# One queue for the opening's transfers, six row buffers, and an earlier third key projection, in a hybrid encoder layer

## The chip, the core and the metric

The kernel runs on one core of a Trainium2 chip. The core has a matrix engine, TensorE (PE in the profile, with its weight loads as PEld), a vector engine (DVE), a scalar engine for activations and copies (ACT), a general engine (POOL, GpSimd), and a sync engine (SP) that mostly issues transfers. Each engine works through its own list of instructions in order; semaphores hold an instruction until its operands are there. Transfers (DMA) between device memory and the on-chip memory can be issued from SP, ACT or POOL, each with its own queue, and sixteen DMA engines carry them out. Matmuls accumulate in PSUM, a small memory from which ACT and DVE must take the results ("evacuate") before a buffer can be used again.

The metric is the time of one execution in device microseconds.

## The reference

One encoder layer is applied to two groups of tokens with the same weights, 256 "prompt" and 512 "sample" tokens, 768 in all, model width 1024. In short:

```python
h = rmsnorm(x, norm_mix_g)
u, q, k, v, qm, gl = split(h @ w_in)
s5_out   = S5 state-space mixer of u, half-GLU
diff_out = differential attention of q, k, v
mem_out  = memory_attention(qm, rmsnorm(mem, mem_norm_g), w_mem_kv)
merged = sum of sigmoid(gl + b_gate) * (branch @ w_branch)
x = x + merged @ w_out
x = x + (silu(g) * up) @ w_down       # h2 = rmsnorm(x), SwiGLU
```

The change concerns the beginning: the normalisation of `mem` (256 memory rows for each group) and of `x`, and the projections of the memory branch. It has four heads of width 256. For head i there is a key projection `("k", i)` and a value projection `("v", i)` of the normalised memory, and a query projection `("q", i)` of the normalised input `h`. All arithmetic is in float32; for the matmuls each operand is split into a high and a low part in a rounded format, and three products of the parts replace one.

## The kernel before

**Weights.** A class `WStream` holds a list of weight blocks in the order in which they are used; a block of 1024 x 256 comes in two halves of 512 KB. `_dma` (line 556) issues one half from SP into one of three raw buffers (`wr`), `_split` (line 650) makes its high part on ACT (`wh`, line 665) and its low part on DVE (`wl`, line 671), into pools of four buffers each, and `get`/`ahead` (lines 673 to 694) keep the stream ahead of use. A raw buffer is free for the next transfer when its low part is made; a `wh` buffer is free when the matmuls that read it are done.

**The order of the memory branch** stands in a list:

```python
MEM_ORDER = [("k", 0), ("k", 1), ("v", 0), ("v", 1), ("q", 0), ("k", 2), ("q", 1), ("v", 2), ("k", 3), ("q", 2),
             ("v", 3), ("q", 3)]
```

`mem_k` (line 929) projects a head's keys with 96 matmuls of 256 columns, in four tiles of tokens, each evacuated by ACT into `kr` (line 940) and squared (line 942). `mem_v` (line 946) first normalises the keys of its head on DVE, then projects the values, with evacuation `Vh`/`Vl` scaled by the row factor `mrs` of the memory. `mem_q` (line 965) projects the queries from the normalised input `H` (tiles `mq`), with 48 matmuls of 256 columns for the prompt and 48 of 512 for the sample, evacuates into `mqh`/`mql`, and transposes the keys (`kT`). Result tiles of these projections take turns in three PSUM buffers (`psd`).

**The opening** (lines 1063 to 1140) is a block of its own:

- `memT`, the transposed memory, comes in four pieces (`mt`, tag `ft`, four buffers) from SP, between the weight halves. It is multiplied by the gain column `gcols` and split into `memThi`/`memTlo` (lines 825, 826); the first key projection runs along with the splitting (line 1088).
- The row factors of the memory need sums of squares of four rows tiles (`load_row`, line 854; squares on DVE, line 1094), and those of the input six (squares on ACT, `square_sum`, line 849, with a separate result tile `njk`). All ten tiles are loaded from POOL's queue into one tag `row` of two buffers.
- `xT`, the transposed input, comes in four pieces (line 1121) from POOL into the same four `ft` buffers as `memT`.
- The input's row factors are spread over all partitions by matmuls (`rsb`, line 1132). Then DVE multiplies `xT` by gain and factor (line 1136), ACT makes `Hhi` (line 822) and DVE `Hlo` (line 823).
- The projections `("k", 1)`, `("v", 0)`, `("v", 1)` are a generator `rest()` whose steps are taken between these parts.

**Behind the opening** a loop (line 1147) goes through `MEM_ORDER[4:]`. It is interleaved with two other generators by `Pace`: `mem_attend` (line 994), the attention of heads whose projections are done, and `s5.params` (line 58), a long chain of small DVE operations on 128 x 64 tiles with a few on ACT, which computes the parameters of the S5 mixer. They advance with each unit of the loop except those of `("q", 0)`. The small tiles of `s5.params` without a name take turns in a ring of 12 buffers. The gate bias `bg` (line 1160) and the gain `subg` (line 1251) are loaded from SP; they are used at lines 1210 and 1261, in later stages.

**What sets the order.** The program is handed to a scheduler that places instructions within each engine's list by its own estimate of time; only those passed through `tc.keep_in_program_order` stay where they are written. So a transfer that waits for nothing can be placed far ahead of the line that issues it. This is why `bg` and `subg` stand eighth and ninth in SP's list.

## Time and profile before

| | |
|---|---|
| median of 3 runs | 1765.29 us (1763.75 to 1769.2) |
| the profiled execution | 1769.52 us, of which its span 1767.7 us |
| PE busy in the span | 1723.5 us (97%) |
| DVE busy | 1341.6 us (76%) |
| ACT busy | 934.6 us (53%) |
| POOL busy | 301.0 us (17%) |
| device memory read, written | 173.51 MB, 52.17 MB |

The span runs from the first to the last instruction of the profiled execution; times in the rows below are microseconds from its start. A row of the windows view gives for a stretch A:B its length, then the busy time of each engine with its number of instructions, the granted TensorE clock (1.00 is full speed), the mean busy share of the sixteen DMA engines, and GB/s. A row in order of time gives start, duration, engine, line, operation, result and operands, and in brackets the idle time of the engine before it with what ended it; "SPq" rows are the queue of SP, whose duration is how long issuing took. A row of the waits view reads: who waited for whom, total, number, longest. Line numbers are those of the kernel before. A matmul's busy time overlaps that of the next, so busy PE is not PE at full flow; counts show that better.

### The profile page before, as it was taken

The page shows a single profiled execution, that of the slowest core. Times are in us where ns is not written, and L with a number is a line of the kernel's source. Part 1 is how long each engine was busy: PE and PEld are TensorE (multiplying, and loading weights), DVE is VectorE, ACT ScalarE, POOL GpSimd, SP SyncE. Part 2 cuts the span into 40 slices and gives each one's busy share as a digit, 9 for nine tenths or more (in the row PEclk, how much of TensorE's full clock was granted, in tenths as well). Part 3 has the DMA queues.
Part 4 walks back from the last instruction along what each step waited for, and adds up shares of the span by engine and source line. Part 5 has one row for each costly group of instructions (what it writes and reads, how often), then busy time and mean ns, then how long its engine had stood idle before and what let it go on. Part 6 is the DMA issues. An engine that isn't in the chain of part 4 may idle for free.

```text
span 1767.7 us, 29778 instructions
## 1 busy us (share of the span) xinstructions
PE 1723.5 (97%) x11312; PEld 1589.3 (90%) x11312; DVE 1341.6 (76%) x2453; ACT 934.6 (53%) x1909; POOL 301.0 (17%) x324
## 2 busy tenths in 40 slices
PE   7699999999999999999999999999999999999999
PEld 7699988888888899999988899898889898989897
DVE  3786575899899645898976687895578868787866
ACT  4535453667566436778866554553334544444541
POOL 1000000000000001011110020350023333443420
PEclk8899999999999999999999999999999999999999
DMA  8412245676666525666594255564303546575743
GB/s 269 155 51 96 90 146 153 148 178 179 165 174 172 146 83 122 142 150 137 145 221 129 93 168 185 148 157 164 104 25 96 149 108 170 139 170 131 167 121 111
DMA packets 202174, 249.90 MB, mean 141 GB/s; under 512 B 33584, under 2 KB 155472, under 8 KB 202032
## 3 DMA queue, kind: packets, MB, share of 16 engines
q1 hardware_dynamic: 156496, 147.18, 27.3%
q0 software_dynamic: 34592, 75.67, 21.1%
q10 hardware_dynamic: 10944, 25.17, 4.1%
q8 instruction: 89, 1.46, 0.3%
q14 instruction: 53, 0.43, 0.1%
HBM read 173.51 MB, written 52.17 MB: 128 GB/s over the span
## 4 chain that ended last, share of the span: by engine, by line
PE 76%; issue 15%; DMA 3%; DVE 3%; ACT 2%; POOL 1%; SPq 0%; POOLq 0%; DVEq 0%; ACTq 0%
PE br L831 4%; PE br L830 4%; PE br L832 4%; PE up L830 3%; PE up L831 3%; PE up L832 3%; PE gate L831 3%; PE gate L830 3%; PE gate L832 3%; PE dn L830 3%; PE dn L831 3%; PE dn L832 3%; PE qk L832 3%; PE qk L830 3%; PE qk L831 3%
## 5 line engine op out<-in xcount | busy, mean ns | idle before, releaser
L665 ACT ACTIVATE wh<-wr 128x1024 fp32r<-128x1024 f32 x118 | 133.8, 1135 | 79.0 <-PE gl L831 19.2
L671 DVE TENSOR_TENSOR wl<-wr,wh 128x1024 fp32r<-128x1024 f32 x72 | 96.2, 1337 | 74.0 <-ACT wh L665 72.3
L830 PE MATMUL gl<-Hhi,wh 128*128 128x256 f32 (+1 forms) x384 | 133.2, 347 | 0.0
L832 PE MATMUL gl<-Hhi,wl 128*128 128x256 f32 (+1 forms) x384 | 129.4, 337 | 0.0
L831 PE MATMUL gl<-Hlo,wh 128*128 128x256 f32 (+1 forms) x384 | 129.4, 337 | 0.0
L669 POOL DMA_DIRECT2D wl<-wr x46 | 40.1, 881 | 465.2 <-ACT wl L668 452.0
L830 PE MATMUL qk<-wh,Hhi 128*128 128x256 f32 x384 | 108.1, 282 | 0.0
L831 PE MATMUL qk<-wl,Hhi 128*128 128x256 f32 x384 | 108.0, 281 | 0.0
L832 PE MATMUL qk<-wh,Hlo 128*128 128x256 f32 x384 | 107.7, 281 | 0.0
L590 DVE TENSOR_TENSOR wl_S<-ws,wh_S 128x512 fp32r<-128x512 f32 x91 | 67.4, 763 | 27.0 <-ACT wh_S L585 26.7
L585 ACT ACTIVATE wh_S<-ws 128x512 fp32r<-128x512 f32 x91 | 54.1, 625 | 63.4 <-PE up L831 27.0
L830 PEld LDWEIGHTS gl<-Hhi,wh 128*128 128x128 f32 x384 | 72.2, 188 | 10.2 <-issue 2.2
L832 PEld LDWEIGHTS gl<-Hhi,wl 128*128 128x128 f32 x384 | 72.3, 188 | 9.2 <-issue 0.6
L831 PEld LDWEIGHTS gl<-Hlo,wh 128*128 128x128 f32 x384 | 72.4, 188 | 7.5
L830 PEld LDWEIGHTS qk<-wh,Hhi 128*128 128x128 f32 x384 | 72.1, 188 | 0.9
L832 PEld LDWEIGHTS qk<-wh,Hlo 128*128 128x128 f32 x384 | 72.2, 188 | 0.5
L831 PEld LDWEIGHTS qk<-wl,Hhi 128*128 128x128 f32 x384 | 72.2, 188 | 0.5
L1378 DVE TENSOR_REDUCE nm<-sc 128x1 f32<-128x512 f32 (+1 forms) x96 | 56.8, 599 | 14.6 <-PE sc L1373 13.8
L1380 ACT ACTIVATE p<-sc,nm 128x512 f32<-128x512 f32 (+1 forms) x96 | 59.0, 617 | 11.0 <-DVE nm L1378 10.6
L611 POOL TENSOR_TENSOR ws<-wr,ws 128x512 f32<-128x512 f32 x26 | 39.9, 1536 | 123.4 <-DVE wl_S L590 119.7
L585 ACT ACTIVATE wh_A<-wr 128x512 fp32r<-128x512 f32 x65 | 38.0, 623 | 37.1 <-PE up L831 16.0
L590 DVE TENSOR_TENSOR wl_A<-wr,wh_A 128x512 fp32r<-128x512 f32 x57 | 51.8, 931 | 6.4 <-ACT wh_A L585 6.4
(705 smaller groups left out, 6244.6 us busy)
## 6 DMA issues: line engine op xcount, KB each, us to landing
wr<-in_w_in_dram SPq DMA_DIRECT2D x48, 512.0 KB, 4.5
wl<-wr POOLq DMA_DIRECT2D x46, 512.0 KB, 5.4
wr<-in_w_gate_up_dram SPq DMA_DIRECT2D x44, 512.0 KB, 4.3
wr<-in_w_branch_dram SPq DMA_DIRECT2D x24, 512.0 KB, 3.5
wr<-in_w_down_dram SPq DMA_DIRECT2D x22, 512.0 KB, 4.6
wr<-in_w_mem_kv_dram SPq DMA_DIRECT2D x16, 512.0 KB, 3.7
wr<-in_w_in_dram SPq DMA_DIRECT2D x32, 256.0 KB, 4.4
p_scr<-de ACTq DMA_DIRECT2D x27, 256.0 KB, 3.9
```

The source lines that it names most:

```text
L585: self.nc.scalar.activation(f(hi), src, AF.Copy)
L590: self.nc.vector.tensor_tensor(out=f(lo), in0=src, in1=f(hi).bitcast(F32), op=ALU.subtract)
L611: gt(out=s4, in0=A12, in1=s2, op=sub)
L665: self.nc.scalar.activation(hi, r, AF.Copy)
L669: self.nc.gpsimd.dma_start(lo, r.bitcast(F32R), accum_op=ALU.add)
L671: self.sub.tensor_tensor(out=lo, in0=r, in1=hi.bitcast(F32), op=ALU.subtract)
L830: pe.matmul(ps, wh, xh, start=start, stop=False)
L831: pe.matmul(ps, wh, xl, start=False, stop=False)
L832: pe.matmul(ps, wl, xh, start=False, stop=stop)
L1378: v.tensor_reduce(out=nm[:, m : m + 1], in_=ps, axis=AX.X, op=ALU.max, negate=True)
L1380: act.activation(pm[:, 0:n], ps, AF.Exp, bias=nm[:, m : m + 1], accum_out=s1s[:, tt : tt + 1] if m == 0 else s2)
```

## The change

- The rows, `xT` and the two gains `gk`, `gq` are issued from SP and not from POOL; `gcols` from ACT. The transfers of the opening, including the weight halves in it (`W.pin`), stay in program order. `bg` and `subg` stay in program order too, so they are issued behind the projections and in the stage of the differential attention.
- The weight stream is brought to four halves ahead of the memory rows. The memory rows are loaded together, before the keys of head 0 are evacuated, and squared behind that.
- A row goes either to the two buffers `row` or to one of the four `ft` buffers. The square of an input row is written over the row itself.
- `("k", 2)` stands ahead of `("q", 0)` and belongs to the opening's generator. `kr` has three buffers instead of two.
- The matmuls that spread the row factors are kept in program order.
- To make room, the ring of `s5.params` has 9 buffers instead of 12, and three of its named tiles share the space of others (`dt` with `ldt`, `thr` with `th`, `p8i` with `xr`).
- The tile `ones2` is filled by DVE instead of POOL.

```diff
@@ S5.params
-            return scratch.tile([128, w], dt, name=nm, tag="ring", bufs=12)
+            return scratch.tile([128, w], dt, name=nm, tag="ring", bufs=9)
-        dt = t("dt")
+        dt = ldt
-        thr = reduce_2pi(t("thr"), th)
+        thr = reduce_2pi(th, th)
-        p8i, p8r = sincos(th8, t("p8i"), t("p8r"))
+        p8i, p8r = sincos(th8, xr, t("p8r"))
@@ WStream
+        self.pin = lambda i: i
-            self.nc.sync.dma_start(tv[:, :, n * j : n * j + n], a[:, k2 * h : k2 * h + k2, :])
+            self.pin(self.nc.sync.dma_start(tv[:, :, n * j : n * j + n], a[:, k2 * h : k2 * h + k2, :]))
@@ hybrid_block
-    MEM_ORDER = [("k", 0), ("k", 1), ("v", 0), ("v", 1), ("q", 0), ("k", 2), ("q", 1), ("v", 2), ("k", 3), ("q", 2),
+    MEM_ORDER = [("k", 0), ("k", 1), ("v", 0), ("v", 1), ("k", 2), ("q", 0), ("q", 1), ("v", 2), ("k", 3), ("q", 2),
-    def square_sum(x, pool, ss):
-        jk = pool.tile([128, 1024], F32, name=uid("njk"), tag="njk", bufs=1)
-        return act.activation(jk, x, AF.Square, accum_out=ss)
-    def load_row(pool, src, eng):
-        x = pool.tile([128, 1024], F32, name=uid("row"), tag="row", bufs=2)
-        eng.dma_start(x, src)
+    def square_sum(x, ss):
+        return act.activation(x, x, AF.Square, accum_out=ss)
+    def load_row(pool, src, ft):
+        if ft:
+            x = pool.tile([128, 2 * TOK], F32, name=uid("row"), tag="ft", bufs=4)[:, 0:1024]
+        else:
+            x = pool.tile([128, 1024], F32, name=uid("row"), tag="row", bufs=2)
+        W.pin(nc.sync.dma_start(x, src))
         return x
-        kr = k1.tile([128, 4, 256], F32, name=uid("kr"), tag="kr", bufs=2)
+        kr = k1.tile([128, 4, 256], F32, name=uid("kr"), tag="kr", bufs=3)
+        W.pin = pin = tc.keep_in_program_order
+        nc.scalar.dma_start(cg, A["gcols"])
-        gp.memset(ones2, 1.0)
+        v.memset(ones2, 1.0)
+        def features(src, n):
+            def load(j):
+                t = pool.tile([128, 2 * TOK], F32, name=uid("ft"), tag="ft", bufs=4)
+                t = t[:, 0 : 2 * n].rearrange("p (k t) -> p k t", k=2)
+                pin(nc.sync.dma_start(t, src[:, 2 * j : 2 * j + 2]))
+                return t
+            return load
+        mt, xt = features(A["memT"], 512), features(A["xT"], TOK)
         W._dma()
-        mt = []
-        for j in range(4):
-            if j == 2:
-                W._dma()
-            t = pool.tile([128, 2 * TOK], F32, name=f"mt{j}", tag="ft", bufs=4)
-            t = t[:, 0:1024].rearrange("p (k t) -> p k t", k=2)
-            nc.sync.dma_start(t, A["memT"][:, 2 * j : 2 * j + 2])
-            if j == 0:
-                nc.gpsimd.dma_start(cg, A["gcols"])
-            mt.append(t)
+        fm = [mt(0), mt(1)]
+        W._dma()
+        fm += [mt(2), mt(3)]
...
+        while W.n_dma < 4:
+            W._dma()
+        rm = [load_row(pool, ms[t], t > 1) for t in range(4)]
         W.get()
         mss = sm.tile([128, 4], F32, name="msq", tag="kss")
-        for t in range(4):
-            xm = load_row(pool, ms[t], nc.gpsimd)
-            tc.keep_in_program_order(v.scalar_tensor_tensor(out=xm, in0=xm, scalar=1.0, in1=xm, op0=mul,
-                                                            op1=mul, accum_out=mss[:, t : t + 1]))
-        nc.gpsimd.dma_start(gk, A["mem_k_g"][0].unsqueeze(0).to_broadcast([128, 256]))
-        gq = pg.tile([128, 256], F32, name="gq")
-        nc.gpsimd.dma_start(gq, A["mem_q_g"][0].unsqueeze(0).to_broadcast([128, 256]))
         for _ in mem_k(0, pss):
             pass
+        for t in range(4):
+            pin(v.scalar_tensor_tensor(out=rm[t], in0=rm[t], scalar=1.0, in1=rm[t], op0=mul,
+                                       op1=mul, accum_out=mss[:, t : t + 1]))
+        pin(nc.sync.dma_start(gk, A["mem_k_g"][0].unsqueeze(0).to_broadcast([128, 256])))
+        gq = pg.tile([128, 256], F32, name="gq")
+        pin(nc.sync.dma_start(gq, A["mem_q_g"][0].unsqueeze(0).to_broadcast([128, 256])))
...
-            for what, h in MEM_ORDER[1:4]:
+            for what, h in MEM_ORDER[1:5]:
...
         for tt in range(TILES):
-            xr = load_row(pool, xs[tt], nc.gpsimd)
-            tc.keep_in_program_order(square_sum(xr, pool, ss[:, tt : tt + 1]))
-            if tt % 3 == 2:
+            if tt in (2, 4):
                 next(units)
-        xt = []
-        for j in range(4):
-            t = pool.tile([128, 2 * TOK], F32, name=f"xt{j}", tag="ft", bufs=4).rearrange("p (k t) -> p k t", k=2)
-            nc.gpsimd.dma_start(t, A["xT"][:, 2 * j : 2 * j + 2])
-            xt.append(t)
+            pin(square_sum(load_row(pool, xs[tt], tt in (2, 3)), ss[:, tt : tt + 1]))
+        fx = [xt(0), xt(1)]
+        next(units)
+        fx += [xt(2), xt(3)]
+        next(units)
...
-                pe.matmul(ps[:, 128 * t : 128 * t + 128], ones2, dg, start=True, stop=True)
+                pin(pe.matmul(ps[:, 128 * t : 128 * t + 128], ones2, dg, start=True, stop=True))
...
+        W.pin = lambda i: i
-    for what, h in MEM_ORDER[4:]:
+    for what, h in MEM_ORDER[5:]:
-    nc.sync.dma_start(bg, A["b_gate"][0].rearrange("(m p) -> p m", p=128))
+    tc.keep_in_program_order(nc.sync.dma_start(bg, A["b_gate"][0].rearrange("(m p) -> p m", p=128)))
-    nc.sync.dma_start(subg, A["diff_sub_g"][0].unsqueeze(1))
+    tc.keep_in_program_order(nc.sync.dma_start(subg, A["diff_sub_g"][0].unsqueeze(1)))
```

4 lines of the change are left out of this document (2 added, 2 removed).

## The prediction

> **What bounds the kernel now.** I read the head of the page first, then the windows of ten microseconds, then the waits and the order of time inside the windows that stand out.
>
> ```profile
> span 1767.7 us, 29778 instructions
> PE 1723.5 (97%) x11312; PEld 1589.3 (90%) x11312; DVE 1341.6 (76%) x2453; ACT 934.6 (53%) x1909; POOL 301.0 (17%) x324
> PEclk8899999999999999999999999999999999999999
> ```
>
> TensorE (PE) has work for 97% of the span, so a change pays only where PE stands still or runs at a lowered clock. The clock line shows that only the first two of forty slices, some 88 us, are below 9 tenths. That is the stretch which the change rebuilds.
>
> ```profile
> core 0: us, PE busy (x) PEld busy (x) DVE busy (x) ACT busy (x) POOL busy (x), PEclk, DMA share, GB/s
> 10.00:20.00 10.00, 7.52 (x49) 6.89 (x49) 4.07 (x6) 4.02 (x7) 1.58 (x6) 0.85 1.01 371
> 20.00:30.00 10.00, 6.31 (x50) 5.90 (x48) 2.87 (x4) 1.74 (x3) 0.53 (x1) 0.98 1.04 284
> 30.00:40.00 10.00, 8.77 (x50) 8.77 (x51) 4.74 (x6) 6.69 (x20) 1.05 (x2) 0.66 0.66 213
> 40.00:50.00 10.00, 10.00 (x87) 10.00 (x87) 4.97 (x8) 4.63 (x9) 0.53 (x2) 1.00 0.45 142
> 80.00:90.00 10.00, 3.30 (x11) 2.69 (x12) 10.00 (x12) 6.74 (x8) 0.00 (x0) 0.50 0.01 4
> ...
> 8.10:120.30 112.20, 89.19 (x622) 83.91 (x621) 74.55 (x223) 52.40 (x102) 7.31 (x18) 0.88 0.49 161
> 120.30:147.60 27.30, 25.54 (x158) 22.63 (x157) 21.14 (x91) 12.96 (x32) 0.00 (x0) 0.94 0.18 59
> 147.60:242.50 94.90, 92.69 (x661) 86.50 (x660) 61.56 (x172) 50.19 (x105) 3.82 (x18) 0.98 0.34 112
> ```
>
> The reader is to see the counts. At full flow PE issues 87 matmuls of 256 columns in 10 us, 0.115 us each. Between 10 and 40 us it issues about 50 per window, between 80 and 90 eleven. Busy time alone hides part of this: in 30 to 40 us PE is "busy" 8.77 us for work of 50 x 0.115 = 5.8 us, because the granted clock is 0.66.
>
> From the first projection matmul (8.1 us) to the start of the second query projection (120.3 us) PE has to do three key and two value projections (480 matmuls), the first query projection (48 narrow and 48 double-width, 144 units), twelve score matmuls, and about thirty small ones of 0.1 us: 636 x 0.115 + 3 = 76 us. It takes 112.2. So **36 us are lost there**, the most that this part can give. The next row, up to the start of the third value projection at 147.6 us, holds about 23 us of work in 27.3, and the row after it 92.7 busy in 94.9.
>
> What ends the waits in the opening:
>
> ```profile
> 4.80 3.58 SPq L1160 DMA_DIRECT2D bg<-in_b_gate_dram  x1
> 8.42 14.87 SPq L1251 DMA_DIRECT2D subg<-in_diff_sub_g_dram  x1
> 23.41 15.86 SPq L566 DMA_DIRECT2D wr<-in_w_mem_kv_dram  x5
> ...
> 4.18 1.06 ACT L665 ACTIVATE wh<-wr 128x1024 fp32r<-128x1024 f32 x1 [2.15 <-DMA wr<-in_w_mem_kv_dram]
> 14.70 1.06 ACT L665 ACTIVATE wh<-wr 128x1024 fp32r<-128x1024 f32 x1 [3.92 <-DMA wr<-in_w_mem_kv_dram]
> 19.14 1.33 ACT L825 ACTIVATE memThi<-mt,gcols 128x512 fp32r<-128x512 f32 x2 [1.84 <-DMA mt<-in_memT_dram]
> 30.12 1.06 ACT L665 ACTIVATE wh<-wr 128x1024 fp32r<-128x1024 f32 x1 [1.00 <-DMA wr<-in_w_mem_kv_dram]
> ...
> 31.23 0.58 PE L830 MATMUL mk<-wh,memThi 128*128 128x256 f32 x1 [4.23 <-ACT wh L665]
> ```
>
> SP issues the gate bias and the sub-layer gain (`bg`, `subg`), which nothing needs for hundreds of microseconds, as eighth and ninth transfers, and is held by them from 4.80 to 23.3 us. The second half of the second key weights comes out only behind them, and PE waits 4.23 us for it.
>
> ```profile
> POOL row L856 <- DVE row L1094: 25.7, 3, 13.3
> ...
> 54.30 1.06 ACT L852 ACTIVATE njk<-row 128x1024 f32<-128x1024 f32 x1 [7.21 <-DMA row<-in_x_prompt_dram]
> 69.09 1.06 ACT L852 ACTIVATE njk<-row 128x1024 f32<-128x1024 f32 x1 [2.40 <-DMA row<-in_x_sample_dram]
> 79.48 7.52 DVE L1136 SCALAR_TENSOR_TENSOR xt<-xt,gcols,rsb 128x768 f32<-128x768 f32 x8 [0.94 <-ACT rsb L1133]
> 86.92 7.04 DVE L823 TENSOR_TENSOR Hlo<-xt,Hhi 128x768 fp32r<-128x768 f32 x8
> 87.93 0.58 PE L831 MATMUL mq<-Hlo,wh 128*128 128x256 f32 x1 [5.28 <-DVE Hlo L823]
> 137.04 0.75 DVE L823 TENSOR_TENSOR mql<-mq,mqh 128x256 fp32r<-128x256 f32 x2
> ```
>
> Ten rows pass through two buffers, one by one (POOL waits 25.7 us for buffers); the last square is at 69.09, so the normalisation of `H` starts at 79.48 and the first query projection can run only from 87.93.
>
> **The change, part by part.** *Queue and order.* The rows and `xT` move from POOL's queue to SP's, `gcols` to ACT's, `bg` and `subg` back to where they are written. Up to the second half of the first query weights (the built program sends the `xT` pieces ahead of it) SP now moves 12 weight halves, 4 pieces of `memT` and 10 rows of 0.52 MB each, 4 pieces of `xT` of 0.79 MB and two gains of 0.13: 13.6 + 3.15 + 0.26 = 17.0 MB. For the rate I take the whole of 8 to 31.2 us:
>
> ```profile
> 8.00:31.20 23.20, 15.78 (x111) 14.46 (x109) 8.36 (x11) 8.08 (x13) 2.30 (x7) 0.92 1.02 333
> ...
> wr<-in_w_mem_kv_dram SPq DMA_DIRECT2D x16, 512.0 KB, 3.7
> ```
>
> The first half lands by 4.18, so with 0.52 MB at 333 GB/s the stream starts at 2.6. Then, each as 2.6 + MB / 0.333: the last `memT` piece (3.1 MB) lands at 12, the row squared last for the memory norm (6.8 MB) at 23, the last `x` row (12.3 MB) at 40, the last `xT` (15.5 MB) at 49, the query weights (17.0 MB) at 54. PE's own pace needs: second half of the first key weights at 8.1 + 48 x 0.115 = 13.6 (it lands at 9, and conversion takes 1.06 + 1.23); `memT` likewise; second key weights at 19 (land at 15); the first value weights at 30 (land at 25). So the two key projections run without a gap, PE's queue of ready work being the cover. The floor is a wait of nothing; the upper price comes from the 284 GB/s of the row 20 to 30: everything then lands a sixth later, the query weights at 62.5.
>
> *Six buffers.* Rows use two own buffers and the four of `memT`/`xT`. The last row at 40 us gives the row scales at 44 (a square of 1.06 and about fourteen small DVE steps). PE reaches the small scale matmuls inside the second value projection, at 8.1 + 4 x 11.0 = 52; their copies end at about 56. DVE must also convert the query weights first (54 + 1.06 + 1.23 = 56.3). Normalisation therefore starts at **56.8** instead of 79.48, and the first `Hlo` is ready 8.4 later, at 65.2. These two limits coincide: beyond this, each microsecond by which the stream is late is one on PE.
>
> *Third key projection first.* It is 96 x 0.115 = 11 us of work which needs no `H`. PE ends five projections and the scale matmuls at 8.1 + 55.2 + 1.5 = 65, just when `Hlo` appears. The first query projection (16.6) and scores (1.4) follow: the second query projection starts at 83 to 86. I add 2 us for short waits and take 86 against 120.3, **a lead of 34 us**.
>
> *What is late next.* The key projection covered something where it stood: DVE's chain for the S5 parameters (about 130 small operations in one dependent line, on the queue in front of the evacuations of the second query projection). In the row of 137.04 DVE gets to that evacuation 57.6 us after normalisation starts. How much of that is work:
>
> ```profile
> 93.95:137.04 43.09, 43.09 (x310) 40.28 (x309) 36.04 (x178) 18.98 (x45) 0.79 (x3) 1.00 0.18 58
> ...
> 113.76 1.28 ACT L138 ACT_TABLE_LOAD   x1
> ```
>
> After normalisation (14.5 us) DVE is busy 36.0 of 43.1 us. With the same operations and no waits it gets there at 56.8 + 14.5 + 36.0 = 107.3; with the waits of before at 56.8 + 57.6 = 114.4. PE would be there at 86 + 11 = 97 and has three result buffers; the fourth tile must wait. So part of the lead is handed back. Before, the third value projection starts 10.6 us after that evacuation; at least 7 of it are needed (24 double-width matmuls and twelve of attention). The bounds for its start are 107.3 + 7 = 114.3 and 114.4 + 10.6 = 125.0. I take the middle, 119.6, since waits on PE fall away but the built program switches ACT's function tables twice more in this stretch (2 x 1.28 us). **Lead at that point: 147.6 - 119.6 = 28 us, bounds 22.6 and 33.3.**
>
> *The rest.* `bg` now stands before the first write of `u` (254.50 before):
>
> ```profile
> 266.58 0.38 SPq L566 DMA_DIRECT2D wr<-in_w_in_dram  x1
> 287.90 2.21 ACT L665 ACTIVATE wh<-wr 128x1024 fp32r<-128x1024 f32 x1
> ```
>
> Should it hold SP for 3.58 + 14.87 us again, from 253 to 271, weights due out at 266.58 go out at 272; they are converted after 287.90. That cover is 12 us; without it the 5 us would fall on PE. The smaller ring of scratch tiles, 12 to 9, and the reused names (`xr`, `th`, `dt`) concern tiles written and read almost wholly by DVE, in its own order: nothing, at most the 1 or 2 us already inside the bounds. One more `kr` buffer only removes a wait. Behind the third query projection the built program has the same order as before on PE but for names; 94.9 us with 92.7 busy leave at most 2 us either way, and I take 0.
>
> Sum against this execution: 1769.52 (its span 1767.7 and 1.8 around it) less 28 is 1741.5. It was 4.2 us above the median of 1765.29; the same 28 us from the median give **1737.3, and I say 1738**.
>
> A rule that would change the sum: the Trainium skill ("TensorE: Matmul & The Clock Gate", "What's actually happening") says that the array falls to half clock when idle and needs about 3.4 us of activity to get it back. The trace agrees in kind (0.50 in the row 80 to 90). By it, a wait of 8 us in the second query projection would cost PE some 1.7 us more afterwards, an estimate from that page; the sum would be 1739.
>
> **The rivals.**
>
> *The stream starves.* One queue carries everything. At 284 GB/s the query weights land at 62.5, normalisation starts at 65, and the DVE bound moves with it: gain 28 - 8 = 20, 1745. At 250 they land at 70.6 and normalisation starts at 73: gain 12, 1753. For it: the row 20 to 30. Against: 371 in the row before.
>
> *DVE hands back all it can.* Evacuation at 114.4 and both table switches in line: 125 + 2.6, gain 20, 1745.
>
> *DVE doesn't decide.* If the evacuations go ahead of the chain, the lead of 34 stays: 1731. Against: 36 us of DVE work stand before them.
>
> *Slower.* Transfers on one queue could be served one after another, each with its whole landing time of 3.7 us. The stream of 17.0 MB is 32 such transfers: 119 us, the query weights at 122, normalisation at 124 instead of 79.5. DVE's chain moves with it, and 28 - (124 - 56.8) is 39 us slower: 1804. It decides from where normalisation starts 28 + 5 us after 56.8, at 90: the query weights at 87.5, 17.0 MB in 85 us, below 200 GB/s on that queue. Against: six transfers issued by 4.2 us landed by 19 while POOL's queue took part of the rate. The Trainium skill ("DMA: Bandwidth & Descriptors", "Anatomy of one DMA — SWDGE (gpsimd) path") gives each transfer 2.0 us fixed plus its bytes over 436 GB/s; for 0.52 MB an estimate of 3.2 us, in series 102 us. The rows above show transfers overlapping, which that formula leaves open.
>
> *It does not do what it says.* If SP's hold of 18 us was only the full stream, not `bg`, the weights stay late and only the buffers help: the loss before 31 us stays (111 matmuls, 12.8 us, in the 23.2 us of the row 8 to 31.2: 10 us), gain 18, 1747.
>
> **How the numbers follow.** Forecast (gain 22 to 33, 1732 to 1743) 0.60; DVE hands all back 0.13; stream starves or hold unexplained 0.14; DVE doesn't decide 0.07; slower 0.05, a stream in between 0.01. The range 1729 to 1750 leaves out the slower case and the worst of the starved ones. A measurement of this kernel tells 0.3%, 5.3 us, from no change: faster 0.91, same 0.04 (a stream of 200 to 228 GB/s, by the same sum), slower 0.05.
>
> **What would show it.** Right: matmul counts near 87 in every window from 10 to 80 us; no SP issue above 4 us before 20 us; the first normalisation step near 57; the second query projection starting near 86; a PE wait of 5 to 12 us before its fourth tile, with DVE fully busy; the third value projection near 120. Wrong: waits of ACT on weights or rows from DMA in the first 55 us; DVE waiting on the query weights before normalisation; PE waiting on weights after `bg` near 225 us.

## The result, and the profile after

| | before | changed |
|---|---|---|
| median | 1766.26 us (4 runs, 1763.75 to 1769.2) | 1741.51 us (4 runs, 1739.09 to 1741.74) |
| profiled execution, its span | 1769.52, 1767.7 | 1741.41, 1739.3 |
| start of the second query projection | 120.32 | 85.71 |
| start of the third value projection | 147.6 | 120.67 |

The ratio of the times is 0.9856, with a 95% interval from 0.9838 to 0.9875. Against the forecast of 1738 us the time is 3.5 us longer; it lies in the range of 1729 to 1750.

The head of the page of the changed kernel, with the clock line:

```profile
span 1739.3 us, 29776 instructions
PE 1713.9 (99%) x11312; PEld 1581.8 (91%) x11312; DVE 1340.6 (77%) x2454; ACT 935.9 (54%) x1911; POOL 292.9 (17%) x306
PEclk9989999999999999999999999999999999999999
```

PE has the same 11312 matmuls. The first two slices of the clock line, 8 and 8 before, are 9 and 9; the third is now the lowest, with 8. Those are the microseconds from 87 to 130, where the change gives something back. The windows of the changed kernel (columns as in the rows of before):

```profile
8.00:31.20 23.20, 23.20 (x199) 23.20 (x199) 20.53 (x45) 16.12 (x34) 0.00 (x0) 1.00 0.97 339
...
100.00:110.00 10.00, 5.80 (x32) 5.33 (x33) 7.59 (x42) 6.41 (x17) 0.00 (x0) 0.80 0.00 1
110.00:120.00 10.00, 8.66 (x32) 6.82 (x31) 8.33 (x31) 4.26 (x9) 0.00 (x0) 0.69 0.08 26
...
85.70:120.70 35.00, 27.72 (x154) 23.95 (x152) 27.63 (x140) 17.28 (x34) 0.00 (x0) 0.85 0.14 41
120.70:215.10 94.40, 92.17 (x671) 86.26 (x670) 62.85 (x178) 51.05 (x111) 3.82 (x18) 1.00 0.36 114
```

From 8 to 31.2 us PE issues 199 matmuls where it issued 111, at full clock, though the transfer rate is nearly the same (339 GB/s for 333). From the second query projection to the third value projection it now takes 35.0 us and not 27.3 for the same work, at a mean clock of 0.85. The stretch behind is as before, 94.4 us for 94.9. The two stretches account for the span: the second query projection starts 34.6 us earlier (120.32 - 85.71), the third value projection 26.9 us earlier (147.6 - 120.67), the end is 28.4 us earlier.

SP's queue of the changed kernel, and the steps that the prediction had times for:

```profile
4.24 8.05 SPq L567 DMA_DIRECT2D wr<-in_w_mem_kv_dram  x3
12.35 0.97 SPq L859 DMA_DIRECT2D row<-in_mem_prompt_dram  x2
```

```profile
55.83 1.21 DVE L672 TENSOR_TENSOR wl<-wr,wh 128x1024 fp32r<-128x1024 f32 x1
56.96 7.52 DVE L1143 SCALAR_TENSOR_TENSOR ft<-ft,gcols,rsb 128x768 f32<-128x768 f32 x8
...
65.80 0.28 PE L831 MATMUL mq<-Hhi,wh 128*128 128x256 f32 x1
...
109.82 0.41 DVE L824 TENSOR_TENSOR mql<-mq,mqh 128x256 fp32r<-128x256 f32 x1
...
120.67 0.36 PE L831 MATMUL mv<-wh,memThi 128*128 128x256 f32 x1
```

Normalisation starts at 56.96 (79.48 before), right behind the conversion of the query weights. The first query projection follows the third key projection at 65.80 without a wait. SP is still held, by 8.05 us on three weight halves, but the order behind it is the order of need, and PE waits for no transfer. `bg`, at its new place (225.34), takes 0.65 us to issue.

What fills the 7.7 us by which the stretch from 85.7 to 120.7 is longer? ACT, PE and DVE in order of time, in the changed kernel:

```profile
96.23 0.26 ACT L138 ACTIVATE sn<-s5t 128x64 f32<-128x64 f32 x1 [5.43 <-DVE s5t L77]
...
98.34 1.28 ACT L1042 ACT_TABLE_LOAD   x1
99.64 0.56 ACT L1042 ACTIVATE mp<-ms,mnm,rqy 128x256 f32<-128x256 f32 x1
...
102.15 0.35 ACT L140 ACTIVATE p8r<-s5t,half_pi 128x64 f32<-128x64 f32 x1
...
104.51 1.28 ACT L1042 ACT_TABLE_LOAD   x1 [1.72 <-DVE mnm L1039]
105.80 0.56 ACT L1042 ACTIVATE mp<-ms,mnm,rqy 128x256 f32<-128x256 f32 x1
```

```profile
100.34 0.38 PE L831 MATMUL ms<-kTh,mqh 128*128 128x256 f32 x1 [2.09 <-ACT mp L1042]
...
104.08 0.44 PE L1054 MATMUL mpT<-ident,mp 128*128 128x128 f32 x2 [1.87 <-DVE mp L1044]
...
106.51 0.58 PE L831 MATMUL ms<-kTh,mqh 128*128 128x256 f32 x1 [1.99 <-ACT mp L1042]
...
112.06 0.80 PE L831 MATMUL mq<-Hhi,wh 128*128 128x512 f32 x1 [1.34 <-ACT mqsq L985]
```

```profile
102.53 0.23 DVE L72 TENSOR_TENSOR fr<-Lr,p8r 128x64 f32<-128x64 f32 x1 [0.65 <-ACT p8r L140]
...
103.68 0.35 DVE L1044 TENSOR_SCALAR mp<-mp,mss 128x256 f32<-128x256 f32 x1
...
104.28 0.15 DVE L1039 TENSOR_TENSOR mnm<-mnm,rqy 128x1 f32<-128x1 f32 x1
```

The reader is to see the order within the lists of ACT and DVE. On ACT the sines of the S5 parameters (`sn`, later `p8r`) wait for DVE's chain, and the exponentials of head 0's softmax (`mp`) stand between them, with a table load at each change of function. On DVE, operations of the chain that need the sines stand between the steps of the same softmax: `fr` waits 0.65 us for `p8r`, and the scaling of `mp` that PE waits for comes behind it at 103.68, though ACT had finished that exponential at 100.84. The third exponential, which needs `mnm` of 104.28 from DVE and another table load, starts at 105.80, 6.2 us after the first. PE waits four times, 7.3 us in all, mostly for `mp`, and runs at a lowered clock behind.

### The profile page after: what moved, and what is told of

Its sections match the earlier page's. It is cut to its first block, busy times and chain, and to the rows that moved or that the text cites. A ratio compares the mean times of both kernels' runs of the same rounds, so it can differ in the third digit from the quotient of the medians.

```text
span 1739.3 us, 29776 instructions
## 1 busy us (share of the span) xinstructions
PE 1713.9 (99%) x11312; PEld 1581.8 (91%) x11312; DVE 1340.6 (77%) x2454; ACT 935.9 (54%) x1911; POOL 292.9 (17%) x306
## 4 chain that ended last, share of the span: by engine, by line
PE 80%; issue 13%; DVE 3%; DMA 2%; ACT 2%; POOL 1%; SPq 0%; POOLq 0%; ACTq 0%; DVEq 0%
PE br L832 4%; PE br L833 4%; PE br L831 4%; PE up L831 3%; PE up L832 3%; PE up L833 3%; PE gate L832 3%; PE gate L833 3%; PE gate L831 3%; PE dn L831 3%; PE dn L833 3%; PE dn L832 3%; PE qk L833 3%; PE qk L831 3%; PE qk L832 3%
## 5 line engine op out<-in xcount | busy, mean ns | idle before, releaser
L1565 DVE TENSOR_TENSOR fs<-fs,up 128x384 f32<-128x384 f32 x70 | 37.5, 548 | 24.0 <-PE up L833 23.2
```

The source lines that it names most:

```text
L1565: v.tensor_tensor(out=o, in0=x, in1=y, op=add)
```

## The experiments

A table of all runs first; "before" is the median of the kernel before on the same chip. The last two columns come from the profile of each.

| run | median | before | ratio (95%) | normalisation | third value projection |
|---|---|---|---|---|---|
| changed kernel | 1741.51 | 1766.26 | 0.9856 (0.9838 to 0.9875) | 56.96 | 120.67 |
| 1: changed, key projection back | 1746.93 | 1768.57 | 0.9879 (0.9854 to 0.9905) | 59.31 | 128.48 |
| 2: changed, `bg`, `subg` early | 1745.67 | 1768.57 | 0.9869 (0.9849 to 0.9888) | 59.54 | 121.74 |
| 3: changed, two row buffers | 1751.37 | 1768.57 | 0.9890 (0.9864 to 0.9915) | 64.47 | 130.69 |
| 4: changed, sines late | 1734.76 | 1768.57 | 0.9811 (0.9789 to 0.9834) | 57.93 | 113.19 |
| 5: before, `bg`, `subg` late | 1761.77 | 1767.81 | 0.9966 (0.9952 to 0.9980) | 73.63 | 141.81 |
| 6: changed, rows and `xT` on POOL | 1747.41 | 1767.81 | 0.9888 (0.9873 to 0.9903) | 63.89 | 127.09 |
| 7: before, key projection first | 1759.85 | 1767.81 | 0.9956 (0.9941 to 0.9971) | 80.81 | 137.82 |
| 8: before, sines late | 1767.13 | 1767.81 | 0.9988 (0.9978 to 0.9999) | 78.14 | 141.99 |
| 9: changed, S5 chain late | 1735.85 | 1766.86 | 0.9829 (0.9801 to 0.9857) | 58.78 | 113.20 |
| 10: changed again | 1742.59 | 1766.86 | 0.9867 (0.9843 to 0.9891) | 57.57 | 119.43 |
| 11: as 4, again | 1735.63 | 1766.86 | 0.9828 (0.9805 to 0.9850) | 57.35 | 112.61 |

### 1. The third key projection put back

```diff
-    MEM_ORDER = [("k", 0), ("k", 1), ("v", 0), ("v", 1), ("k", 2), ("q", 0), ("q", 1), ("v", 2), ("k", 3), ("q", 2),
+    MEM_ORDER = [("k", 0), ("k", 1), ("v", 0), ("v", 1), ("q", 0), ("k", 2), ("q", 1), ("v", 2), ("k", 3), ("q", 2),
-            for what, h in MEM_ORDER[1:5]:
+            for what, h in MEM_ORDER[1:4]:
-    for what, h in MEM_ORDER[5:]:
+    for what, h in MEM_ORDER[4:]:
```

> The changed kernel with the third key projection behind the first query projection again, all else kept. Theory (the projection covers the wait for H at 54 to 65 us where it stands now, and covered the S5 and softmax chain where it stood before): PE waits about 10 us for Hlo after the second value projection (end near 54.5, Hlo near 65), the second query projection starts near 94 and not at 85.7, but from there to the third value projection it takes 27 us as before and not 35. So the third value projection again starts near 121 and the time is 1738 to 1744, no more than 3 us from the changed kernel (1741.5). Rival (the 7 us given back between 86 and 121 us have to do with the queue or the buffers and not with the missing cover): the stretch stays 35 us, the third value projection starts near 129, and the time is 1749 to 1752.

Two windows of this kernel, the wait for `H` and the stretch from the second query projection to the third value projection:

```profile
60.00:70.00 10.00, 3.48 (x11) 2.83 (x12) 10.00 (x12) 6.74 (x8) 0.00 (x0) 0.50 0.17 51
...
100.80:128.50 27.70, 25.93 (x159) 22.63 (x158) 20.76 (x89) 12.90 (x31) 0.00 (x0) 0.94 0.18 58
```

The row from 60 to 70 has the counts of 80 to 90 in the kernel before: eleven matmuls, clock 0.50. The second query projection starts at 100.84, 15.1 us later than in the changed kernel, and not the 8 that was expected: besides the wait for the first `Hlo`, PE goes through the first query projection at the pace at which DVE makes `Hlo`. The second half of the theory held: the stretch takes 27.7 us, as before, and not 35. So 7.3 of the 15.1 us come back, and the third value projection is 7.8 us later than in the changed kernel. The ratio, 0.9879, lies between the two ranges. The profiled execution (1753.49) is the longest of the four, 6.6 us above their median, so its times may be late by a part of that. The place of the key projection decides which of two gaps it fills; it can't fill both.

### 2. `bg` and `subg` eighth and ninth on SP again

```diff
-    tc.keep_in_program_order(nc.sync.dma_start(bg, A["b_gate"][0].rearrange("(m p) -> p m", p=128)))
+    nc.sync.dma_start(bg, A["b_gate"][0].rearrange("(m p) -> p m", p=128))
-    tc.keep_in_program_order(nc.sync.dma_start(subg, A["diff_sub_g"][0].unsqueeze(1)))
+    nc.sync.dma_start(subg, A["diff_sub_g"][0].unsqueeze(1))
```

> The changed kernel with the gate bias and the sub-layer gain unpinned, so that they stand eighth and ninth on SP again. Theory (these two transfers hold SP, and nothing else fills the queue meanwhile): SP is held for about 15 us from 5 us on, the seven transfers ahead (3.6 MB) are done by 13 us and the stream stands idle until about 20, so all behind lands about 10 us later; normalisation of H starts at 66 to 70 instead of 57, PE waits for the second key weights by some 5 us, and the time is 1748 to 1753. Rival (the hold is only the full queue, the bytes flow all the same): SP's issues are long but the last xT piece lands within 2 us of the changed kernel, and the time is 1740 to 1743.

SP's queue, PE's progress, and the transfers of 10 to 15 us: busy share of the DMA engines (in tenths) and rate in forty slices of 0.125 us, then the packets (a packet is one contiguous piece; "under 512 B" counts the small ones). The last fence has the packets of the changed kernel:

```profile
5.44 8.34 SPq L1259 DMA_DIRECT2D subg<-in_diff_sub_g_dram  x1
13.90 0.92 SPq L567 DMA_DIRECT2D wr<-in_w_mem_kv_dram  x2
14.87 1.81 SPq L859 DMA_DIRECT2D row<-in_mem_prompt_dram  x2
```

```profile
8.00:31.20 23.20, 23.20 (x197) 23.20 (x197) 18.05 (x36) 15.88 (x35) 0.00 (x0) 1.00 0.95 303
```

```profile
DMA  9999989899999999999999999999984322101119
GB/s 393 360 393 410 418 336 451 328 361 393 369 369 369 377 344 353 320 281 265 193 154 82 58 50 50 25 9 8 7 6 2 2 1 1 1 1 1 1 1 83
DMA packets 3875, 0.95 MB, mean 191 GB/s; under 512 B 3254, under 2 KB 3776, under 8 KB 3875
```

```profile
DMA packets 1522, 1.82 MB, mean 364 GB/s; under 512 B 53, under 2 KB 1420, under 8 KB 1522
```

The memory's rows go out at 14.87 where the changed kernel sends them at 12.35: most of the hold of 8.34 us is one that SP has anyway. What the small transfers cost is 0.87 MB in these 5 us. The slices show two parts of about 1.1 us each: from 12.6 to 13.75 us the engines are busy at less than 100 GB/s, with the small pieces; from 13.75 to 14.9 they are nearly idle, since SP issued the next weights only at 13.90. So the stream does stand still, as the theory had it, but for 1 us and not for 7. The second half of the second key weights is converted 3.5 us later than in the changed kernel (18.72 for 15.18), and PE doesn't wait for it: 197 matmuls from 8 to 31.2 us, for 199.

The 0.87 MB are 2.6 us at 333 GB/s, and normalisation starts 2.6 us later (59.54). That agreement proves little: in experiments 1, 4, 9, 10 and 11, whose transfers are those of the changed kernel, normalisation starts between 57.35 and 59.31. At the third value projection 1.1 us are left, and the ratio (0.9869) can't be told from the changed kernel's. The theory's ten microseconds are refuted, the rival is nearly right.

### 3. Two row buffers

```diff
-        rm = [load_row(pool, ms[t], t > 1) for t in range(4)]
+        rm = [load_row(pool, ms[t], False) for t in range(4)]
-            pin(square_sum(load_row(pool, xs[tt], tt in (2, 3)), ss[:, tt : tt + 1]))
+            pin(square_sum(load_row(pool, xs[tt], False), ss[:, tt : tt + 1]))
```

> The changed kernel with all ten rows in the two row buffers again. Theory (six buffers matter since a row that waits for its buffer holds all of SP's stream): rows three and four of the memory wait for the squares on DVE behind the first key evacuation (15 us or later), the third and fifth rows of x for a landing and a square each (5 to 6 us), in all 10 to 15 us of hold, of which some is slack; normalisation starts at 64 to 72, time 1747 to 1755. Rival (two buffers were no limit once the order is right): normalisation within 2 us of 57 and 1740 to 1743.

```profile
12.88 0.97 SPq L859 DMA_DIRECT2D row<-in_mem_prompt_dram  x2
20.70 1.47 SPq L859 DMA_DIRECT2D row<-in_mem_sample_dram  x2
...
31.92 1.56 SPq L859 DMA_DIRECT2D row<-in_x_prompt_dram  x2
38.87 7.45 SPq L859 DMA_DIRECT2D row<-in_x_sample_dram  x4
```

As the theory had it: between the second and the third row of each group SP stands still for 5 to 7 us (20.70 - 13.85, 38.87 - 33.48), and the weights behind wait with it. Normalisation is 7.5 us later, the third value projection 10.0. On one queue in order the buffers are worth this much because a row without a buffer holds back everything behind it.

### 4. The sines at their program place

```diff
-            nc.scalar.activation(s, th, AF.Sin)
+            self.tc.keep_in_program_order(nc.scalar.activation(s, th, AF.Sin))
-            nc.scalar.activation(c, a, AF.Sin, bias=env.half_pi, scale=-1.0)
+            self.tc.keep_in_program_order(nc.scalar.activation(c, a, AF.Sin, bias=env.half_pi, scale=-1.0))
```

> The changed kernel with the four sine activations of the S5 parameters pinned to their program place, which is behind the exponentials of head 0's softmax on ACT; now they stand ahead of them and ACT switches its function table five times. Theory A (the 7 us given back between 86 and 121 us are PE waiting for head 0's softmax, whose exponentials stand in ACT's list behind sines that wait for DVE's chain of small operations): PE's waits of 2.1, 1.9 and 2.0 us at 97.9 to 106.5 and the lowered clock behind them go, the third value projection starts at 110 to 115 instead of 120.7, and the time is 1731 to 1737. Theory B (DVE's own work in front of the evacuations binds, as the prediction had it): the third value projection moves by less than 2 us, 1739.5 to 1742. Rival C (the parameters come late for the packing and the u stage): up to 1750.

ACT's exponentials of head 0 and the window of the stretch, in this kernel:

```profile
99.10 0.56 ACT L1042 ACTIVATE mp<-ms,mnm,rqy 128x256 f32<-128x256 f32 x1 [8.62 <-DVE mnm L1039]
...
101.72 0.56 ACT L1042 ACTIVATE mp<-ms,mnm,rqy 128x256 f32<-128x256 f32 x1 [1.41 <-PE mpT L1054]
```

```profile
86.70:113.20 26.50, 24.09 (x154) 20.94 (x153) 21.54 (x91) 11.50 (x29) 0.00 (x0) 1.00 0.19 60
```

What PE itself waited for in this kernel from 85 to 125 us (the waits view: total, number, longest):

```profile
PE mo L831 <- DVE kTl L824: 1.2, 1, 1.2
PE ms L831 <- ACT mp L1042: 1.1, 2, 0.6
```

The third exponential starts at 101.72 instead of 105.80, the clock stays at 1.00, and the stretch takes 26.5 us instead of 35.0. The third value projection starts at 113.19. Theory A's numbers, 110 to 115 and 1731 to 1737, hold; theory B's don't. This version is faster than both kernels, and is so again in run 11.

The edit moves more than the four sines. The DVE operations that need them go with them: DVE has 91 operations in the stretch instead of 140, 21.54 us of work instead of 27.63. So this run doesn't tell the part of the sines on ACT from that of these operations on DVE, and theory B's number took no account of them. (The table loads in the changed kernel's stretch are four, not five: at 89.52, 98.34, 100.86 and 104.51.)

### 5. The kernel before, with `bg` and `subg` late

The two edits of experiment 2 turned round, in the kernel before.

> The kernel before with nothing changed but the gate bias and the sub-layer gain kept at their program place. H comes from 87 us on in any case (rows through two buffers), so the time moves little, 0.997 to 1.001 of before; what tells the theories apart is PE's progress before 40 us. Theory as predicted (these two transfers keep the second key weights away): PE stands at 31 us where it should, about 190 matmuls between 8 and 31.2 us instead of 111. Theory after the second experiment (POOL's queue moves rows and xT at the same time and takes about half of the rate, the weights are late with or without the two): no more than 135 matmuls in that stretch.

```profile
8.00:31.20 23.20, 18.82 (x139) 17.92 (x138) 11.47 (x15) 10.73 (x24) 2.83 (x8) 0.93 0.97 352
```

139 matmuls, between the 111 of before and the 199 of the changed kernel, and just above the bound of 135, so neither theory's number holds: with POOL's queue beside it, the weights stay late without the two small transfers as well. That `H` doesn't move was wrong: normalisation starts 5.9 us earlier (73.63), and the whole kernel gains (0.9966). DVE takes the low parts of the weights and the squares of the memory rows in one list, and these squares free the two row buffers: the second pair starts at 41.55 instead of 47.33, and POOL issues the first input row at 43.08 instead of 48.85.

### 6. Rows and `xT` from POOL

```diff
-        W.pin(nc.sync.dma_start(x, src))
+        W.pin(nc.gpsimd.dma_start(x, src))
-                pin(nc.sync.dma_start(t, src[:, 2 * j : 2 * j + 2]))
+                pin(eng.dma_start(t, src[:, 2 * j : 2 * j + 2]))
-        mt, xt = features(A["memT"], 512), features(A["xT"], TOK)
+        mt, xt = features(A["memT"], 512, nc.sync), features(A["xT"], TOK, nc.gpsimd)
```

> The changed kernel with the rows and xT issued from POOL again (its own queue, in the same order among themselves, six buffers as now), the weights and memT from SP. Theory (what the one queue gives is the order of need: two queues share the rate, and rows and xT that nobody needs yet make the early weights late): PE loses 6 to 12 us before 40 us as before, the first query projection starts 6 to 10 us later than at 65.8, and the time is 1746 to 1751. Rival (all bytes are needed by 57 us, and the order among them is slack): less than 2 us, 1740 to 1743.

```profile
8.00:31.20 23.20, 21.91 (x183) 21.36 (x184) 16.87 (x27) 13.89 (x30) 3.16 (x6) 1.00 0.93 316
```

ACT and DVE of this run, and PE; the last fence has ACT's conversion of the same half in the changed kernel:

```profile
51.11 1.06 ACT L666 ACTIVATE wh<-wr 128x1024 fp32r<-128x1024 f32 x1 [5.55 <-DMA wr<-in_w_mem_kv_dram]
...
52.20 1.23 DVE L672 TENSOR_TENSOR wl<-wr,wh 128x1024 fp32r<-128x1024 f32 x1 [3.22 <-ACT wh L666]
53.34 0.16 DVE L814 SCALAR_TENSOR_TENSOR rqy<-rqt,rqy 128x6 f32<-128x6 f32 x1
...
54.14 1.21 PE L1139 MATMUL rsb<-rsd,ones 128*128 128x128 f32 x4 [2.44 <-DVE rsd L1138]
```

```profile
51.22 1.06 ACT L666 ACTIVATE wh<-wr 128x1024 fp32r<-128x1024 f32 x1 [3.04 <-DMA wr<-in_w_mem_kv_dram]
```

The time (1747.41) is in the theory's range, the place is not quite. The early weights are late, as the theory had it: the second half of the second key weights is converted at 20.51 instead of 15.18. But only 2 us of PE's time are lost before 40 us (183 matmuls in the row, for 199). The larger piece comes later. PE stands at the matmuls that spread the row factors, for 2.44 us. The last step of these factors (`rqy`) stands in DVE's list behind the low part of the last half of the third key weights, for which DVE and ACT wait. That half is no later than in the changed kernel (51.11, 51.22); there the row factors were ready ahead of it, at 48.24. So this piece comes from the order in DVE's list in this build, and not directly from two queues sharing the rate; what put the factors behind isn't settled. Normalisation is 6.9 us later, the third value projection 6.4. The bytes are the same. What is shown for one queue in order of need is the early weights; the rest of the 6 us is this build's.

### 7. The kernel before, with the key projection first

```diff
-    MEM_ORDER = [("k", 0), ("k", 1), ("v", 0), ("v", 1), ("q", 0), ("k", 2), ("q", 1), ("v", 2), ("k", 3), ("q", 2),
+    MEM_ORDER = [("k", 0), ("k", 1), ("v", 0), ("v", 1), ("k", 2), ("q", 0), ("q", 1), ("v", 2), ("k", 3), ("q", 2),
-            for what, h in MEM_ORDER[1:4]:
+            for what, h in MEM_ORDER[1:5]:
-    for what, h in MEM_ORDER[4:]:
+    for what, h in MEM_ORDER[5:]:
```

> The kernel before with only the third key projection put ahead of the first query projection. It fills most of the 13 us in which PE waits for H before 87.9 us, so the second query projection starts 8 to 11 us earlier than at 120.3. Theory (behind it the chain through DVE's parameters, ACT's sines and head 0's softmax ends last, and it starts with H, which is as late as before): the third value projection starts 0 to 4 us earlier than at 147.6, time 0.997 to 1.000 of before. Rival (PE's work alone counts there): 8 to 11 us earlier, 0.994 to 0.9955.

```profile
107.90:137.80 29.90, 25.60 (x153) 22.53 (x152) 26.38 (x130) 15.70 (x33) 0.00 (x0) 0.94 0.15 47
```

```profile
121.04 0.56 ACT L1039 ACTIVATE mp<-ms,mnm,rqy 128x256 f32<-128x256 f32 x1
...
123.00 0.26 ACT L138 ACTIVATE sn<-s5t 128x64 f32<-128x64 f32 x1
```

The theory is refuted, the rival nearly right. The second query projection starts 12.4 us earlier, and the third value projection 9.8, though normalisation is no earlier (80.81). So the 68 us from normalisation to the third value projection in the kernel before (147.6 - 79.48) were not set by a chain that starts with normalisation; here it takes 57.0. In this build two exponentials stand ahead of the sines, and the stretch takes 29.9 us, between the 27.3 of before and the 35.0 of the changed kernel.

### 8. The kernel before, with the sines late

The edit of experiment 4, in the kernel before.

> The kernel before with only the four sines of the S5 parameters at their program place. Theory (the softmax waiting behind the sines costs only where the change has taken the third key projection out of that stretch; before, PE had it to do): PE lost about 2 us there, so 0.998 to 1.000 of before. Rival (the sines cost the same in both orders): 0.994 to 0.997, as the changed kernel gained 7 to 8 us by it.

The ratio is 0.9988, as the theory said: 0.12 points, where the same edit is worth 0.45 in the changed kernel (0.9856 to 0.9811) and 0.39 in the repeat (0.9867 to 0.9828). The sines cost most where the key projection is no longer there to do meanwhile. The profiled execution of this run has the third value projection 5.6 us earlier and a span 4.9 us shorter (1762.8 for 1767.7), more than the ratio's 2 us. It lies 2.5 us below the median of its ten executions, so the ratio is the figure to go by.

### 9. The whole S5 chain late, and 10 and 11, repeats

```diff
                 mat.tick(u_)
-                par.tick(u_)
+                if (what, h) != ("q", 1):
+                    par.tick(u_)
-            xc = tsc(t(), x, -87.0, 88.0, ALU.max, ALU.min)
+            xc = t()
+            self.tc.keep_in_program_order(v.tensor_scalar(out=xc, in0=x, scalar1=-87.0, scalar2=88.0, op0=ALU.max, op1=ALU.min))
```

> The changed kernel with the whole chain of the S5 parameters (DVE's small operations and the four sines) behind the second query projection: its generator does not advance there and its first operation is pinned to its program place. The sines then stand behind the softmax of heads 0 and 1 on ACT. Theory A (what PE waited for was the softmax behind the sines; DVE's small operations themselves cost it little): like the fourth experiment, third value projection at 110.5 to 114, 1731 to 1737. Theory B (DVE's operations in front of the evacuations hold PE besides): 107 to 110, 1727 to 1731. Rival C (the chain in the next stretch is paid there): third value projection early, but the lead is gone by the third query projection, 1737 to 1742.

> The changed kernel itself, on the same chip as the two beside it. All theories: 0.984 to 0.9875 of before, some 7 us above the version with the sines late.

> The version of the fourth experiment (sines of the S5 parameters at their program place) again, beside the changed kernel on the same chip. Theory A: 0.979 to 0.983 of before, 6 to 9 us below the changed kernel, third value projection at 111 to 115. Rival (the first result was chance): within 3 us of the changed kernel.

```profile
87.50:113.20 25.70, 23.87 (x154) 21.04 (x152) 15.63 (x48) 11.54 (x29) 0.00 (x0) 1.00 0.19 62
```

DVE has 48 operations in the stretch, where experiment 4 has 91 and the changed kernel 140. The stretch gets 0.8 us shorter than in experiment 4 (25.7 us for 26.5); the third value projection starts at 113.20, as there. Theory A's numbers hold, and rival C is refuted by the time. So the operations of the chain that stood on DVE ahead of the exponentials cost PE about 0.8 us. The sines and the operations that need them, which stood among the steps of the softmax, cost it 8.5 us (35.0 - 26.5). How these 8.5 us divide between the sines on ACT and the operations on DVE isn't shown: no run moves the one without the other. In the repeats, side by side on one chip, the version with late sines is 7.0 us below the changed kernel (1742.59 - 1735.63).

## Why the prediction was right, and where it was wrong

**The opening: right in time and order.** The stream's rate was taken as 333 GB/s and is 339 from 8 to 31.2 us. Normalisation was put at 56.8 and starts at 56.96, the first query projection was put at 65 and starts at 65.80, the second at 86 and starts at 85.71. The lead there, forecast as 34, is 34.6 us. In the repeat (run 10) normalisation starts at 57.57 and the third value projection at 119.43. The rival of a starved stream and that of transfers served one by one are refuted by the same rows. One sign that was named for "wrong" did show: ACT waits for weights and rows from DMA in the first 55 us, at the most 3.04 us (the conversion at 51.22). PE waits for neither, so the sign was too strict. The row factors, put at 44, were ready at 48.24, and PE still came to the matmuls that spread them without a wait.

**The part of `bg` and `subg`: mostly wrong.** The prediction read SP's hold of 18 us as the cause of the late weights, and costed the hold, if it was not theirs, at a loss of 10 us before 31 us. Experiment 2 brings the two back: the second key weights are 3.5 us later, PE doesn't wait for them, and at the third value projection 1.1 us are left, no more than the 1.2 us by which the changed kernel and its repeat differ there. Alone on the kernel before, moving them gives 5.9 us (experiment 5), but only 28 of the 88 missing matmuls (139 - 111, 199 - 111).

Where the rest lay can be read from the time at which ACT converts the second half of the second key weights: 30.12 in the kernel before, 26.75 without the two small transfers (experiment 5), 20.51 with the changed kernel's order but two queues (experiment 6), 15.18 in the changed kernel. In the kernel before, POOL's queue moved 4.22 of the 7.73 MB from 8 to 31.2 us, most of it `xT`, which normalisation needs only at 79.48; in experiment 6 `xT` goes behind the rows. So moving what is not needed yet was the larger part (44 matmuls between experiments 5 and 6), and two queues at once the smaller (16 between 6 and the changed kernel). No run changes one of these alone in the kernel before, so this split is argued and not shown.

The rival "the hold was only the full stream" was right that SP is held without them too (8.05 us), and wrong that the weights then stay late. "No SP issue above 4 us" was a false sign for the same reason. And `subg` was not as idle as the text ahead of the prediction has it. In the kernel before, ACT's scaling of it (line 1261) stood in the opening too:

```profile
28.92 0.20 ACT L1261 ACTIVATE subg<-subg 128x1 f32<-128x1 f32 x1 [4.79 <-DMA subg<-in_diff_sub_g_dram]
```

It held ACT for 4.79 us ahead of the conversion at 30.12; the weights came 1.00 us later still, so this hold cost nothing more. The Trainium skill ("DMA: Bandwidth & Descriptors", "Issuing engines are not separate DMA queues") says that transfers from different engines' queues share the same sixteen DMA engines and interleave; experiment 6 agrees, with the second key weights 5.3 us later (20.51 for 15.18) for the same bytes on two queues.

**Six buffers and the key projection: right.** Without the buffers the third value projection is 10.0 us later (experiment 3). Without the move of the key projection the second query projection is 15.1 us later, and 7.3 of them come back because the old gap is covered again (experiment 1).

**What is late next: the size right, the mechanism wrong.** The prediction said that the fourth tile of the second query projection must wait for a result buffer, since DVE has the small operations in front of its evacuation. The evacuation came at 109.82, inside the bounds of 107.3 to 114.4, and the third value projection at 120.67 for 119.6. But PE waits only 1.34 us for buffers there; the other three waits, 5.95 us, are for head 0's softmax, whose steps stand among the sines on ACT and among the operations that need the sines on DVE. DVE is busy for 27.63 of 35.0 us, not fully. Two runs bear this out: with the sines and what needs them behind the softmax the stretch falls to 26.5 us, and with the rest of the chain moved too to 25.7. So the step that failed is the wait: not DVE's sum of work in front of the evacuation and a full set of result buffers, but the order of two tasks in the lists of ACT and DVE. How much of it is ACT's and how much DVE's stays open. The 57.6 us "with the waits of before" were no bound of DVE's either: in experiment 7 the evacuation comes 47.9 us after normalisation starts (128.68 - 80.81). That the number fitted is partly luck.

**The clock: named, and larger than said.** The prediction gave 1.7 us, outside its sum, for the clock behind the new waits. Of the 8.5 us between the stretches of the changed kernel and of experiment 4, the waits make 5.0 (7.3 there, 2.3 here from the rows of PE's waits), so about 3.5 us go to the lowered clock, 0.80 and 0.69 in the two windows and 1.00 in experiment 4. The matmuls themselves give the same: from 106.51 on, 18 start 0.213 us apart instead of 0.115, and from 112.06 nine of double width 0.427 instead of 0.233, 1.8 and 1.7 us more. The Trainium skill ("TensorE: Matmul & The Clock Gate", "What's actually happening") puts the half clock down to a window of about 3.4 us without work. The trace agrees as to about half the pace, but no single wait was that long here: the slow matmuls follow two waits of 1.87 and 1.99 us with two small transposes between them.

**The sum: right for the profiled execution, 3 us too large for the median.** Forecast 28, measured 28.1 (1769.52 - 1741.41). The prediction took the same 28 us off the median; the medians differ by 24.75. The profiled execution of before lay 3.3 us above its median, that of the changed kernel 0.1 below. What made that execution longer isn't settled. A part of such scatter shows in the trace between 884 and 903 us of the changed kernel: there its lead over before grows from 26.9 to 28.5 us with the same order of work on both sides, and two executions of the changed kernel (its own and run 10) differ there by 1.8 us. As far as these traces show, 26.9 of the 28.4 us in the span are the change's.

## What to carry to other kernels

Put all loads of an opening on one queue in the order in which they are needed, with enough buffers that none of them has to wait in that queue (two buffers instead of six cost 10.0 us at the third value projection here); a second queue shares the rate and makes the urgent transfer late (by 5.3 us for the second key weights). A block of matmuls that is moved into one gap opens the gap that it covered: look what it hid, on every engine. On an engine that works through its list in order, look for the function of a side task among those that PE waits for; here moving four sines, and with them the operations that need them, behind a softmax was worth more than a quarter of the whole change (7.0 us beside 24.75). A pin on one instruction moves all that depends on it: count the operations on the other engines before putting the gain down to one of them.

## What was not expected of the hardware

Two transfers of 12 KB and 0.5 KB in pieces of 4 bytes took 0.87 MB out of 5 us of the stream (191 GB/s beside 364): for about 1.1 us the DMA engines were busy with the small pieces, and for about 1.1 us more they were nearly idle, since the next transfer was issued late. What that cost the kernel (0.9869 beside 0.9856) isn't clear of the scatter.

A switch of ACT's function table took 1.28 us each time, and the next activation followed directly: load at 98.34, exponential at 99.64. The Trainium skill ("ScalarE: Activation LUTs", "What ACT_TABLE_LOAD costs") gives 1283 ns for the load, which agrees, and about 1380 ns more for a drain, which no row here shows.
